# Local attention in 64-row windows: sending the last unit out in two stores, and asking for its v one store earlier

## The chip, the cores and the metric

One core of one Trainium2 chip. The time is device microseconds of one execution. Runs were "fast" (one core, so the only test is that no run lies over 1.5% above the fastest of its kernel).

## The reference

q, k and v are float32 of shape (4, 4096, 1536). The sequence is cut into windows of 64 rows; each window attends to itself alone.

```python
logits = np.einsum('bnwd,bnud->bnwu', q_w, k_w) * D ** -0.5
attn = np.exp(logits - logits.max(-1, keepdims=True))
attn = attn / attn.sum(-1, keepdims=True)
out = np.einsum('bnwu,bnud->bnwd', attn, v_w)
```

## The kernel before

The 16,384 rows go through in 32 units of 512 rows. Each unit's q, k and v are loaded by GpSimd's queue, cast to float16 on the way, into landing buffers two deep. GpSimd copies them on, and asks for the load two units ahead at each copy ("hand_over"). TensorE transposes q and k, multiplies, ScalarE takes exponentials, TensorE multiplies by v, and VectorE and ScalarE share the evictions, which also divide by the sums. A partition holds four consecutive rows of the unit, 24,576 bytes, which leave in one piece. All stores but the last are issued by GpSimd, on the same queue as the loads; the last is issued by SyncE.

```python
def hand_over(x, u, dst, m, g):
    gp.wait_ge(landed[x][u % NL], ...)      # the load of unit u has landed
    gp.wait_ge(m, u)                        # unit u-1 no longer reads dst
    gp.tensor_copy(out=dst, in_=landing[x][u % NL])
    ...
    request(x, u + NL)                      # NL = 2: the load two units ahead
...
for u in range(1, N):                       # GpSimd
    hand_over("q", u, q16, m_q, g_q)
    hand_over("k", u, k16, m_k, g_k)
    gp.wait_ge(m_q, u + 1)                  # unit u-1 is evicted
    store(u - 1)
    hand_over("v", u, v16, m_v, g_v)

for a in range(2):                          # SyncE: n_e counts the evictions of
    sy.wait_ge(n_e[a], 3)                   # rows 2 and 3 of the last unit
sy.dma_start(out=rows(of, (N - 1) * UR, SLOTS, SLOTS),
             in_=slots(outs[(N - 1) % NO], 0, SLOTS, SLOTS)).then_inc(d_l, 16)
```

The softmax here doesn't subtract the row's maximum and nothing guards it: scores larger than these inputs give would overflow.

## Time and profile before

| | before |
|---|---|
| median of 6 runs | 943.4 us (943.28 to 944.1) |
| span of the profiled run | 941.3 us |
| busiest compute engine (PE) | 68% |
| DMA engines busy | nine tenths or more in 39 of 40 slices |
| HBM read and written | 428 GB/s over the span |
| last eviction ends, last store issued | 929.21, 929.24 us |

The prediction shows the lines themselves (in them PE is TensorE, PEld its weight loads, DVE VectorE, ACT ScalarE, POOL GpSimd and SP SyncE; the granted clock is a share of TensorE's full clock). They are to be read from the DMA row downwards: the compute engines have room to spare, and after the start the only stretch before the end in which most DMA engines have nothing to do is 928 to 930 us (DMA share 0.28).

### The profile page before, as it was taken

How to read it: one execution, taken by the hardware profiler on the slowest of the kernel's cores; microseconds unless marked ns; L12 is line 12 of the kernel's file. 1: busy time of each engine (PE TensorE's matmuls, PEld its weight loads, DVE VectorE, ACT ScalarE, POOL GpSimd, SP SyncE). 2: the span in 40 equal slices, each digit the busy share in tenths (PEclk: the TensorE clock that was granted, in tenths of full speed). 3: DMA queues.
4: the chain of work that ended last, by engine and by line, in shares of the span. 5: the costliest groups of instructions: out<-in, count | busy, mean ns of one | idle time of the engine just before them, and what ended most of it. 6: DMA issues, size and time to landing. Idle time of an engine off the chain costs nothing. (4 is left out here: it accounts for less than half of the span.)

```text
span 941.3 us, 13141 instructions
## 1 busy us (share of the span) xinstructions
PE 641.9 (68%) x5120; PEld 371.9 (40%) x3584; DVE 288.4 (31%) x517; ACT 336.0 (36%) x642; POOL 334.1 (35%) x225
## 2 busy tenths in 40 slices
PE   0877777666767767768676586676866767757673
PEld 0544444432444433444233442344533444323440
DVE  0233333332323333233322233222333223322232
ACT  0344444333333233333333333333334334233331
POOL 4244433344333342333423334333343333443220
PEclk9999999998889888797888999889789789888997
DMA  9999999999999999999999999999999999999997
GB/s 257 217 216 279 264 237 282 284 279 276 233 275 283 281 281 237 266 282 282 281 245 257 283 281 282 255 246 283 283 280 264 237 284 283 280 277 230 276 320 329
DMA packets 22540, 253.35 MB, mean 269 GB/s; under 512 B 2048, under 2 KB 2048, under 8 KB 10240
## 3 DMA queue, kind: packets, MB, share of 16 engines
q0 software_dynamic: 22240, 246.95, 99.7%
q1 hardware_dynamic: 288, 6.29, 1.7%
q14 instruction: 10, 0.08, 0.0%
q8 instruction: 2, 0.03, 0.0%
HBM read 301.99 MB, written 100.66 MB: 428 GB/s over the span
## 5 line engine op out<-in xcount | busy, mean ns | idle before, releaser
L164 PE MATMUL lt<-xq,xk 128*128 128x256 f16 x1536 | 203.3, 282 | 0.0
L300 POOL COPY v<-vl 128x3072 f32<-128x3072 f32 x31 | 85.2, 2748 | 278.3 <-DMA vl<-in_v_dram 278.3
L192 PEld LDWEIGHTS <-et 128*64 128x64 f16 x512 | 40.5, 131 | 331.6 <-issue 319.4
L152 PE MATMUL tp<-ident,k 128*128 128x128 f32 x768 | 124.9, 297 | 57.9 <-PEq L218 40.5
L164 PEld LDWEIGHTS lt<-xq,xk 128*128 128x128 f16 x1536 | 153.2, 100 | 27.3
L152 PE MATMUL tp<-ident,q 128*128 128x128 f32 x768 | 107.9, 285 | 80.1 <-DVE xq L228 55.8
L112 PE MATMUL sp<-ones,et 128*64 128x1 f16 x512 | 52.6, 178 | 147.8 <-PEq L218 130.6
L152 PEld LDWEIGHTS tp<-ident,q 128*128 128x128 f32 x768 | 85.9, 145 | 120.8 <-issue 120.7
L228 ACT COPY xk<-tp 128x512 f32<-128x512 f32 x96 | 59.6, 620 | 203.2 <-ACTq L218 203.2
L152 PEld LDWEIGHTS tp<-ident,k 128*128 128x128 f32 x768 | 96.0, 152 | 75.1 <-issue 73.1
L300 POOL COPY k<-kl 128x3072 f32<-128x3072 f32 x31 | 85.2, 2748 | 103.1 <-DMA kl<-in_k_dram 103.1
L245 DVE RECIPROCAL rs<-sp 128x1 f32<-128x1 f32 x128 | 21.4, 167 | 323.8 <-DVEq L218 323.2
L300 POOL COPY q<-ql 128x3072 f32<-128x3072 f32 x31 | 85.0, 2743 | 100.0 <-DMA ql<-in_q_dram 99.9
L228 DVE COPY xk<-tp 128x512 f32<-128x512 f32 x96 | 66.5, 693 | 168.2 <-DVEq L218 168.2
L112 PE MATMUL o<-v,et 128*64 128x512 f16 x768 | 117.7, 440 | 0.0
L279 ACT ACTIVATE out<-tp,rs 128x512 f32<-128x512 f32 x64 | 44.0, 687 | 177.4 <-ACTq L218 177.4
L269 ACT ACTIVATE et<-lt,zeros 32x128 f16<-32x128 f32 x256 | 92.0, 359 | 39.4 <-ACTq L218 36.1
L228 ACT COPY xq<-tp 128x512 f32<-128x512 f32 x96 | 56.3, 586 | 126.4 <-ACTq L218 126.4
L112 PE MATMUL tp<-v,et 128*64 128x512 f16 x512 | 100.2, 468 | 0.0
L256 DVE TENSOR_SCALAR out<-o,rs 128x512 f32<-128x512 f32 x128 | 90.4, 747 | 28.6 <-DVEq L218 28.6
L228 DVE COPY xq<-tp 128x512 f32<-128x512 f32 x96 | 66.1, 688 | 83.7 <-DVEq L218 83.7
L112 PE MATMUL lt<-v,et 128*64 128x512 f16 x256 | 64.5, 479 | 0.0
(21 smaller groups left out, 217.6 us busy)
## 6 DMA issues: line engine op xcount, KB each, us to landing
out_dram<-out POOLq DMA_DIRECT2D x31, 3072.0 KB, 61.6
ql<-in_q_dram POOLq DMA_DIRECT2D x31, 1536.0 KB, 54.9
kl<-in_k_dram POOLq DMA_DIRECT2D x31, 1536.0 KB, 54.9
vl<-in_v_dram POOLq DMA_DIRECT2D x31, 1536.0 KB, 54.9
out<-in_q_dram SPq DMA_DIRECT2D x1, 3072.0 KB, 16.7
out_dram<-out SPq DMA_DIRECT2D x1, 3072.0 KB, 10.7
k<-in_k_dram POOLq DMA_DIRECT2D x1, 1536.0 KB, 17.9
v<-in_v_dram POOLq DMA_DIRECT2D x1, 1536.0 KB, 24.3
```

The lines of the kernel that those rows point to most:

```text
L112: return nc.tensor.add_instruction(mybir.InstMatmult(name=nc.get_next_instruction_name(), engine=PE, ins=[low(rhs), low(w)], outs=[low(o)] ...
L152: ins = nc.tensor.transpose(tps[g % 2][:, r, j, :], pairs[:, c * P : (c + 1) * P], ident[:, :])
L164: ins = nc.tensor.matmul(lts[h][:, r, :, :], lhsT=keys(c, h, r, w), rhs=queries(c, h, w), start=(c == 0 and w == 0 and r == 0), stop=(c == ...
L192: ld = nc.tensor.ldweights(w[h], tile_position=(0, P // H * h))
L228: copy(out=dst, in_=tps[g % 2][:, :, :, :]).then_inc(f_c[g % 4], 1)
L245: ve.reciprocal(out=rs[:, n : n + 1], in_=sp[:, n : n + 1]).then_inc(n_d, 1)
L256: ins = ve.tensor_scalar_mul(scaled(u, n, j), bank(n, j), scalar1=rs[:, n : n + 1])
L269: ins = sc.activation(ets[h][s, :, :, t], lts[h][s, :, :, t], EXP, bias=zeros[s, 0:1], scale=scale)
L279: ins = sc.activation(scaled(u, n, j), bank(n, j), COPY, bias=0.0, scale=rs[:, n : n + 1])
L300: gp.tensor_copy(out=dst[:, :, :].bitcast(FP32), in_=landing[x][u % NL][:, :, :].bitcast(FP32)).then_inc(c_l, 1)
```

## The change

The intent is to close that stretch in two ways. The last unit's v is requested ahead of a store that stood in front of it in the queue, so that the last unit can be computed sooner; and the first two rows of the last unit go out while the last two are still computed. The diff, cut to its core:

```diff
         for u in range(1, N):
             hand_over("q", u, q16, m_q, g_q)
             hand_over("k", u, k16, m_k, g_k)
+            if u + NL == N - 1:
+                hand_over("v", u, v16, m_v, g_v)
             gp.wait_ge(m_q, u + 1)
             store(u - 1)
-            hand_over("v", u, v16, m_v, g_v)
-        for a in range(2):
-            sy.wait_ge(n_e[a], 3)
-        sy.dma_start(
-            out=rows(of, (N - 1) * UR, SLOTS, SLOTS), in_=slots(outs[(N - 1) % NO], 0, SLOTS, SLOTS)
-        ).then_inc(d_l, 16)
+            if u + NL != N - 1:
+                hand_over("v", u, v16, m_v, g_v)
+        last = rows(of, (N - 1) * UR, SLOTS, SLOTS)[:, 0, :]
+        for i, c in enumerate((1, 3)):
+            for a in range(2):
+                sy.wait_ge(n_e[a], c)
+            sy.dma_start(
+                out=last[:, 2 * i * D : 2 * (i + 1) * D],
+                in_=outs[(N - 1) % NO][:, 2 * i : 2 * (i + 1), :].rearrange("p r d -> p (r d)"),
+            ).then_inc(d_l[i], 16)
```

(`d_l` becomes two semaphores, and the end waits for both.)

More of the change, by code (lines that the diff above doesn't have):

```diff
@@ L76 @@
     d_o = [sem(f"d_o{i}") for i in range(NO)]
-    d_l = sem("d_l")
+    d_l = [sem(f"d_l{i}") for i in range(2)]
     g_q, g_k, g_v = (sem(n) for n in ("g_q", "g_k", "g_v"))
@@ L381 @@
             sy.wait_ge(d_o[i], 16 * (last // NO + 1))
-        sy.wait_ge(d_l, 16)
+        for i in range(2):
+            sy.wait_ge(d_l[i], 16)
         lo, hi = min(s.num for s in sems), max(s.num for s in sems)
```

## The prediction

> **What bounds the kernel now.** I read the page first, for the occupancy of each engine and of the DMA engines, then the page's DMA queues and issues.
>
> ```profile
> PE 641.9 (68%) x5120; PEld 371.9 (40%) x3584; DVE 288.4 (31%) x517; ACT 336.0 (36%) x642; POOL 334.1 (35%) x225
> ...
> DMA  9999999999999999999999999999999999999997
> ...
> q0 software_dynamic: 22240, 246.95, 99.7%
> q1 hardware_dynamic: 288, 6.29, 1.7%
> ...
> HBM read 301.99 MB, written 100.66 MB: 428 GB/s over the span
> ```
>
> No compute engine is above 68%, while the 16 DMA engines are full in 39 of 40 slices. This is a copy-bound kernel: each unit of 512 rows moves three loads and one store of 3.15 MB each, and the steady rhythm in the timeline is 29.3 us a unit (v copies at 829.34, 858.61, 887.90). So what matters is only when the DMA engines have nothing to do. That can be at the start, which the change leaves alone, and at the end. I therefore cut the end into stretches (columns: stretch, its length, busy us of PE, PE weight load, DVE, ACT, POOL, granted clock, DMA share, GB/s).
>
> ```profile
> 25.00:925.00 900.00, 637.61 (x5088) 369.94 (x3570) 284.16 (x507) 332.29 (x637) 323.45 (x211) 0.89 1.02 269
> 925.00:928.00 3.00, 2.67 (x28) 0.40 (x6) 1.89 (x6) 1.63 (x4) 0.00 (x0) 1.00 0.94 401
> 928.00:930.08 2.08, 0.00 (x0) 0.00 (x0) 1.21 (x2) 0.49 (x1) 0.00 (x0) 1.00 0.28 118
> 930.08:937.50 7.42, 0.00 (x0) 0.00 (x0) 0.00 (x0) 0.00 (x0) 0.00 (x0) 0.59 0.99 418
> 937.50:938.60 1.10, 0.00 (x0) 0.00 (x0) 0.00 (x0) 0.00 (x0) 0.00 (x0) 0.50 0.16 67
> ```
>
> The reader sees a hole: from 928 to 930.08 the DMA share drops to 0.28, because the queue of earlier work runs dry and the last store is not yet issued. The timeline of the same place says why:
>
> ```profile
> 902.45 2.75 POOL L300 COPY k<-kl 128x3072 f32<-128x3072 f32 x1 [4.52 <-DMA kl<-in_k_dram]
> ...
> 905.82 0.54 POOL L285 DMA_DIRECT2D out_dram<-out  x1 [0.62 <-POOL k L300]
> ...
> 915.38 2.98 ACT L269 ACTIVATE et<-lt,zeros 32x128 f16<-32x128 f32 x8 [1.13 <-ACTq L218]
> 917.14 2.75 POOL L300 COPY v<-vl 128x3072 f32<-128x3072 f32 x1 [10.78 <-DMA vl<-in_v_dram]
> 920.05 0.14 PEld L192 LDWEIGHTS <-et 128*64 128x64 f16 x2 [4.18 <-issue]
> ...
> 926.21 0.75 DVE L256 TENSOR_SCALAR out<-tp,rs 128x512 f32<-128x512 f32 x1 [0.45 <-DVEq L218]
> 926.22 0.69 ACT L279 ACTIVATE out<-tp,rs 128x512 f32<-128x512 f32 x1 [1.04 <-ACTq L218]
> ...
> 927.80 1.41 DVE L256 TENSOR_SCALAR out<-o,rs 128x512 f32<-128x512 f32 x2 [0.45 <-DVEq L218]
> 927.81 0.69 ACT L279 ACTIVATE out<-o,rs 128x512 f32<-128x512 f32 x1 [0.32 <-ACTq L218]
> 929.24 0.35 SPq L373 DMA_DIRECT2D out_dram<-out  x1
> ```
>
> The last v lands at 917.1, is copied, the second product starts at 920.05, its last eviction ends at 927.80 + 1.41 = 929.21, and only then does the one 3 MB store go out.
>
> The share is an average over 16 engines, so I went to the records of the single DMA packets. A packet of 24,576 B takes 0.91 us; each engine has 8 of a store. Between 25 and 925 us I find no idle moment on any of the 16 engines (longest gap 0.08 us). At the end they part. The 16 closing records of the last software-queue store come at 927.84, 927.95, 927.96 and so on; the 13th at 929.89, the 14th and 15th at 930.36 and 930.37, the 16th at 931.61. The last store's packets start at 930.08. So 13 engines stand idle before it, for 0.18 to 2.37 us, 22.3 engine-microseconds together; three engines never stand idle. The one that finishes its old work at 931.61 ends the program: 13 of the last store's closing records fall in 937.41 to 937.57, two at 938.18 and 938.45, and this engine's at 939.46; the issue view has 10.7 us from issue to landing, so landing at 939.94. This engine did not catch up during the hole, because it had no hole: its lag on the quickest is 1.75 us at 19 us, 2.52 at 500 and 3.77 at 931.6.
>
> **What the Trainium skill says.** "DMA: Bandwidth & Descriptors", section "Issuing engines are not separate DMA queues", says that transfers issued from different engines run on the same 16 DMA engines and interleave. The trace agrees: the hardware-queue packets follow the software-queue ones on the same chains. The same page, "Queues, rings and completion order", says that each DMA engine takes turns between its queues at packet granularity; around 930.4 two packets that overlap a software-queue one last 1.46 and 1.73 us instead of 0.91, which fits. Its section "Why a DMA increments its semaphore by 16 and not by 1" says that only the full 16 means that all data have landed. That is the core of this prediction: the latest engine counts, not the mean. Its section "Latency and other measured facts" says that two of the engines are usually slower in traces; the trace shows one that trails, though the records carry no engine number to compare.
>
> **The change part by part.**
>
> (1) *The last v asked for ahead of a store.* In the unit whose v copy starts at 858.61, GpSimd now issues the load of the last v (861.95 before) ahead of the store that it issued at 847.75. The software queue is served in order and is some 55 us deep (median landing of loads 54.9 us), so the late issue does not starve it; the two transfers change places. Each takes 7.3 us of queue (8 x 0.91), so the last v lands near 909.8 instead of 917.1. What then holds the product is the exponentials: they end at 915.38 + 2.98 = 918.36, against the v copy's 917.14 + 2.75 = 919.89. The gain is 920.05 - 918.4 = 1.6 to 1.7 us on the last eviction, not 7.3. The displaced store lands 7.3 us later, at about 917.2, and the first eviction of the last unit needs its buffer; that would be at 921.86 - 1.6 = 920.2, so about 3 us are in hand.
>
> (2) *The last store in two.* The first half waits for the first evictions of row 2 (926.21 + 0.75 = 926.96, and 926.22 + 0.69 = 926.91) instead of 929.21, so 2.25 us earlier, with part (1) at about 925.3. From the start of issue to the first packet it took 930.08 - 929.24 = 0.84 us, so first packets come near 926.2, before the quickest engine runs dry at 927.84. The second half is ready near 927.6, with packets near 928.5; by then the first half's 8 packets of about 0.46 us (3.65 us) are still being worked off until 927.84 + 3.65 = 931.5. So the hole closes completely: 22.3 engine-microseconds of idleness vanish.
>
> (3) *What it costs.* Each engine gets 16 packets of 12,288 B instead of 8 of 24,576. From v loads, whose packets read 12,288 B and take 0.47 us, 16 x 0.47 = 7.5 against 8 x 0.91 = 7.3, so 0.2 us on every engine. One more store issue (0.35 us) on SyncE falls while transfers run; one more satisfied wait at the end is an estimate of under 0.1 us.
>
> *The sum.* On the quick engines, the end moves from 937.5 to 927.84 + 7.5 = 935.3, a gain of 2.2. On the slowest, which sets the time, no idleness is removed: 931.61 + 7.5 = 939.1. Before, it ended at 939.47, which is 931.61 + 7.3 plus about 0.58: an instruction fetch of 8,192 B at 933.43 (0.31 us) and the packet after it that took 1.18 us. If the fetch comes again at this engine, 939.1 becomes 939.7; if not, or if the work is ordered more kindly, 939.1. Against 939.47 that is -0.4 to +0.2. I put the middle, -0.15, on the median: 943.36 - 0.15 = 943.2.
>
> **The rivals.** *The hole is on the path.* Then the time falls by up to 2.2 us, to about 941.2, and with a second-slowest engine at the end something between. For it: DMA share of 0.28 just before the last store. Against it: the three engines that end last were not idle there. It would hold if in unprofiled runs the engines trailed less than in the profile; but to have even 1 us of gain the slowest must finish its old work by 929.1, which is 2.5 us earlier than here, and then the unprofiled runs of before would be faster than the profiled one. They are 943.29 to 944.1, the profiled 943.07. *The displaced store becomes a wait.* If it lands over 3 us later than worked out, evictions of the last unit start late and the second half goes out late. Even 2 us would still be covered by queued transfers (the slowest has work until 931.61), so the time stays within 0.5 us, 943.9 at most. *Smaller packets or sharing cost more than the loads show*: at twice my overhead, +0.2 us more, 943.6. *The load order pays 7.3 us*: this would need the last unit's chain to begin with v; the exponentials at 918.36 speak against it, and the total of bytes still has to pass: at best the same 941.2.
>
> **Range and chances.** The mechanism gives 942.9 to 943.6; runs of before spread by 0.8 us, and a partial gain of the first rival is possible, so 942.3 to 944.1. Two per cent would be 18.9 us, more than eight times the length of the hole; so 98% within it.
>
> **What would show it.** Right: the DMA share near 1.0 between 928 and 930 instead of 0.28, two SyncE stores about 2.2 us apart with the first near 925.3, the second product starting near 918.4 and the last v copy near 909.9; then a ragged end, most engines done near 935.3 to 937.8 with the share falling from about 935, one alone to 939.1 to 939.7; span 940.9 to 941.5. Wrong: a span under 940, with no engine trailing alone by over 2 us at the end; or a hole that is still there; or the last unit's evictions waiting on their buffer, which would be a start after 921.

## The result, and the profile after

The changed kernel takes 943.7 us in the median of 6 runs (943.44 to 943.84), the kernel before 943.4 (943.28 to 944.1) on the same chip: ratio 1.0001, 95% interval 0.9988 to 1.0014. Ratios here are the mean time of one kernel's fast runs over that of the other's in the same rounds, so not quite the ratio of the medians. There is no difference that these runs can see.

And yet the profile shows that the change did all that it was meant to do. First the timeline of the changed kernel (start, length, engine, line, operation, idle time before it and what ended that):

```profile
909.92 2.75 POOL L300 COPY v<-vl 128x3072 f32<-128x3072 f32 x1 [3.43 <-DMA vl<-in_v_dram]
...
917.48 0.20 PE L112 MATMUL sp<-ones,et 128*64 128x1 f16 x2 [2.31 <-ACT et L269]
...
924.86 2.56 SPq L379 DMA_DIRECT2D out_dram<-out  x2
...
925.65 1.41 DVE L256 TENSOR_SCALAR out<-o,rs 128x512 f32<-128x512 f32 x2 [0.45 <-DVEq L218]
```

The last v is copied from 909.92 instead of 917.14, and the last product, no longer waiting for v but for the exponentials ("ACT et"), starts at 917.48 instead of 920.20 (its first weights, at 920.05 in the prediction's line, are loaded from 917.41). The last eviction ends at 927.06 instead of 929.21, and the first half of the last unit goes out at 924.86, 4.4 us before the whole store of the kernel before. Now the stretches of the end, in the columns of the prediction's view:

```profile
925.00:928.00 3.00, 0.52 (x6) 0.00 (x0) 1.58 (x3) 1.02 (x2) 0.00 (x0) 0.97 0.95 410
928.00:930.08 2.08, 0.00 (x0) 0.00 (x0) 0.00 (x0) 0.00 (x0) 0.00 (x0) 0.50 0.97 414
930.08:935.00 4.92, 0.00 (x0) 0.00 (x0) 0.00 (x0) 0.00 (x0) 0.00 (x0) 0.50 1.01 429
935.00:937.50 2.50, 0.00 (x0) 0.00 (x0) 0.00 (x0) 0.00 (x0) 0.00 (x0) 0.50 0.37 157
937.50:938.60 1.10, 0.00 (x0) 0.00 (x0) 0.00 (x0) 0.00 (x0) 0.00 (x0) 0.50 0.08 34
938.60:941.70 3.10, 0.00 (x0) 0.00 (x0) 0.00 (x0) 0.00 (x0) 0.00 (x0) 0.50 0.02 8
```

The hole is gone: the DMA share between 928 and 930.08 is 0.97, where it was 0.28. The idle time has moved to the other side of the store, where it is of no use to anyone: from 935 on the share is 0.37, then 0.08, then 0.02, which is a third of one engine of 16. In the records of the single packets, 15 engines end between 935.40 and 937.58, and one at 939.92; before, 15 ended between 937.42 and 938.45, and one at 939.46. The quick engines gained up to 2 us. The slow one gained nothing, and the kernel ends with it. (The records carry no engine number. But a packet's record starts 3 to 4 ns before the record ahead of it on its engine ends, and a record of 4 bytes, the "closing record", ends each engine's share of a transfer; by these two marks the packets can be chained. Times are counted from the same zero as in the views.)

### The profile page after: what moved, and what is told of

The parts are those of the page before. It is cut to its first block, busy times and chain, and to the rows that moved or that the text cites. A ratio compares the mean times of both kernels' runs of the same rounds, so it can differ in the third digit from the quotient of the medians.

```text
span 941.7 us, 13144 instructions
## 1 busy us (share of the span) xinstructions
PE 644.9 (68%) x5120; PEld 373.5 (40%) x3584; DVE 288.3 (31%) x517; ACT 335.5 (36%) x642; POOL 334.2 (35%) x225
```

## The experiments

The theory on trial, S: every DMA engine has its own list of work, no engine is idle in the middle of the kernel, and the end is that of the engine with the longest list. Its rivals: C, closing the hole does gain 2 us but the change gives them back elsewhere; H, the hole is on the path, and any shift of the last store shifts the end; M, the sum of bytes over all engines sets the end. Each run below had five rounds beside the kernel before, whose medians on these chips were 943.06 to 943.56 us.

### Each part alone: split_only and order_only

split_only: the order of the requests as before, the last store in two.

```diff
-            if u + NL == N - 1:
-                hand_over("v", u, v16, m_v, g_v)
             gp.wait_ge(m_q, u + 1)
             store(u - 1)
-            if u + NL != N - 1:
-                hand_over("v", u, v16, m_v, g_v)
+            hand_over("v", u, v16, m_v, g_v)
```

> The last store in two halves, the last v not moved ahead. Theory S (the DMA engine that trails the others and never stands idle sets the end): the first half goes out near 927.0, the hole shrinks to little or nothing, and the time stays at 943.4 to 943.8, since the trailing engine's last packet stays near 939.5 to 939.9. Rival C (closing the hole does gain 2 us, and the displaced store of the other part gives it back): 941.3 to 942.0.

order_only: the other way round, in the kernel before.

```diff
+            if u + NL == N - 1:
+                hand_over("v", u, v16, m_v, g_v)
             gp.wait_ge(m_q, u + 1)
             store(u - 1)
-            hand_over("v", u, v16, m_v, g_v)
+            if u + NL != N - 1:
+                hand_over("v", u, v16, m_v, g_v)
```

> The last v ahead of a store, the last store whole. Theory S: the store goes out about 2 us earlier (near 927.2, as the last evictions in the changed kernel end at 927.06), the hole shrinks to a few tenths, and the time stays at 943.1 to 943.7. Rival C, now with the cost in the smaller packets of the two halves: without them the gain of 1.5 to 2 us would show, 941.5 to 942.0.

Measured: split_only 943.1 us, ratio 1.0000 (0.9986 to 1.0014); order_only 943.51 us, ratio 1.0005 (0.9992 to 1.0019). The store's issue and one stretch of order_only:

```profile
925.05 0.35 SPq L376 DMA_DIRECT2D out_dram<-out  x1
```

```profile
928.00:930.08 2.08, 0.00 (x0) 0.00 (x0) 0.00 (x0) 0.00 (x0) 0.00 (x0) 0.50 1.02 441
```

This is the plainest case. One whole store, with the packets of the kernel before, goes out 4.2 us earlier (925.05 against 929.24; I had expected 2, the exponentials and evictions of this run were early too), the hole is fully closed, and the slowest engine ends at 939.68 against 939.46. (It was 0.49 us further back at the closing of the store before, 924.55 against 924.05.) In split_only the hole is closed to a share of 0.82:

```profile
928.00:930.08 2.08, 0.48 (x6) 0.00 (x0) 1.58 (x3) 0.99 (x2) 0.00 (x0) 1.00 0.82 349
```

Its slowest engine ends at 939.10, and its median is 0.3 us under the range given for S, within the noise. Rival C falls: neither part has a gain that the other could give back.

### The last store later: late6 and late6_changed

If the slowest engine still has old work when the store's packets come, a later store must cost nothing at first and then cost one for one. late6 puts six evictions that no one needs between VectorE's last eviction and the last store of the kernel before.

```diff
+        if u == N - 1:
+            for i in range(6):
+                ve.tensor_scalar_mul(
+                    xq[:, i, :], bank(H * R - 1, NJ - 1), scalar1=rs[:, 3:4]
+                ).then_inc(n_e[0], 1)
...
-            sy.wait_ge(n_e[a], 3)
+            sy.wait_ge(n_e[a], 3 if a else 9)
```

> The kernel before with six idle evictions of about 0.7 us on VectorE put between its last eviction and the last store, so the store goes out 4.2 us later and the hole is made 4.2 us wider. Theory S: the trailing engine had 931.61 - 930.08 = 1.5 us of old work left when the store's packets came, so only 4.2 - 1.5 = 2.7 us reach the time: 945.8 to 946.4. Rival H (the hole is on the path for all engines): the full 4.2 us, 947.5.

Measured: 946.77 us, ratio 1.0035 (1.0022 to 1.0049), which is 3.3 us (2.1 to 4.6); the medians on this chip are 3.7 us apart. That is 0.4 us above the range given for S. The delay as the timeline has it, and two stretches:

```profile
930.28 4.03 DVE L262 TENSOR_SCALAR xq<-o,rs 128x512 f32<-128x512 f32 x6
...
934.34 0.35 SPq L378 DMA_DIRECT2D out_dram<-out  x1
```

```profile
930.08:935.00 4.92, 0.00 (x0) 0.00 (x0) 4.23 (x7) 0.00 (x0) 0.00 (x0) 0.75 0.02 10
935.00:937.50 2.50, 0.00 (x0) 0.00 (x0) 0.00 (x0) 0.00 (x0) 0.00 (x0) 0.50 1.12 472
```

In this run the evictions before the added ones were also about 1.1 us later, so the store went out 5.1 us later than in the kernel before, not 4.2. H then says 5.1; S says 5.1 less the 1.5 us of old work, 3.6. The time agrees with S and excludes 5.1, if the other executions had the delay of the profiled one; the 4.2 us that H had been given beforehand it would not exclude. The packets decide: the slowest engine closed its old work at 931.94, all 16 then stood idle until 935.18 (DMA share 0.02), and its first packet of the store came 3.56 us later than in the kernel before (931.62), not 5.1. The other 15 end within 942.53 to 942.66, and one at 943.24.

late6_changed puts the same six evictions before the second half of the changed kernel.

```diff
-                sy.wait_ge(n_e[a], c)
+                sy.wait_ge(n_e[a], c if a or c == 1 else 9)
```

(and the six evictions as above)

> The changed kernel with the same six idle evictions (4.03 us on VectorE in the earlier run) ahead of its second half. The half goes out near 926.3 + 4.0 = 930.3 to 931.5, its packets come near 931 to 932.5. Theory S: the trailing engine still works on old packets and the first half until about 931.6 + 3.7 = 935.3, so nothing of the delay reaches the time: 943.3 to 944.0. Rival H, that whatever delays the last store delays the end: 947 to 948, as in the delayed kernel before, which rose by 3.3 us.

Measured: 943.52 us, ratio to the kernel before 0.9999 (0.9986 to 1.0013). Beside it on the same chip the changed kernel ran once more.

> The changed kernel once more, as the partner of the next run on the same chip: 943.3 to 943.9, the slowest engine's last packet 2 us or more after the second slowest.

It took 943.6 us (ratio 1.0001), its slowest engine ended at 940.31 and the second slowest at 937.93. The delay in late6_changed, and the stretch at the hole:

```profile
926.28 6.51 SPq L384 DMA_DIRECT2D out_dram<-out  x2
```

```profile
928.00:930.08 2.08, 0.00 (x0) 0.00 (x0) 2.08 (x4) 0.00 (x0) 0.00 (x0) 0.79 0.86 366
930.08:935.00 4.92, 0.00 (x0) 0.00 (x0) 2.34 (x4) 0.00 (x0) 0.00 (x0) 0.50 0.92 389
```

The row of the issues spans both halves, from 926.28 to 932.79. The same delay that cost the kernel before 3.3 us costs the changed one nothing. In the packet records eleven engines wait for the second half and go on at 933.28 to 933.43, while those of the slowest engine follow each other without a gap from 927.01 to its end. (The profiled execution was the slowest of its five, 944.91 us; the other four were 943.23 to 943.53. Its slowest engine was 1.0 us behind that of after_again at the closing of the store before, 926.03 against 925.03, so before the delay could act.) So the change is not without effect: what it bought is slack of four microseconds or more for the last evictions, of which this kernel had no need.

### More work for some of the engines: one8 and low4

If the longest list sets the end, a little work on one engine must cost nearly its full length. one8 adds eight loads of one row at the start, into the third output buffer, which is free until unit 2.

```diff
+        src = rows(qf, 0, SLOTS, SLOTS)[:, 0, :]
+        for i in range(8):
+            nc.sync.dma_start(
+                out=outs[2][i : i + 1, :, :].rearrange("p r d -> p (r d)"),
+                in_=src[i : i + 1, :],
+            ).then_inc(d_x, 16)
```

(and a wait for them before that buffer is given free)

> The changed kernel with eight extra loads of one row of 24,576 B each at the start, into a buffer that is not in use yet: meant for one DMA engine alone, 8 x 0.91 = 7.3 us of extra work on it, 0.08% of all bytes. Theory S (the engine with the most work sets the end, and the lag persists because no engine is ever idle): that engine ended at 935.4 to 937.5 if it is not the trailing one (939.88), so it now ends at 942.7 to 944.8 and the time rises by 2.8 to 5 us, to 946.5 to 948.7; by 7.3 us to 951 if it is the trailing one. Rival M (the sum over all engines sets the end): 7.3 / 16 = 0.5 us, 944.2.

Measured: 946.07 us, ratio 1.0028 (1.0014 to 1.0042), 2.6 us above the kernel before and 2.4 above the changed one's earlier median: 0.4 us under the lowest value of S, five times the value of M. The issue, and the end of one8:

```profile
out<-in_q_dram SPq DMA_DIRECT2D x8, 24.0 KB
```

```profile
937.50:940.00 2.50, 0.00 (x0) 0.00 (x0) 0.00 (x0) 0.00 (x0) 0.00 (x0) 0.50 0.12 49
940.00:944.00 4.00, 0.00 (x0) 0.00 (x0) 0.00 (x0) 0.00 (x0) 0.00 (x0) 0.50 0.05 22
```

Two engines of 16 are left after 937.88, one to 941.14 and one to 942.47. Nine hundred microseconds after those eight rows were loaded, their 7.3 us were still missing on one engine: 942.47 less the 7.4 us that the last store takes is 935.1, and the quickest engine closed its old store at 927.77, 7.3 us before. Nothing in the kernel lets an engine catch up, because its list never runs empty. That 0.08% more bytes cost 0.28% is not to be explained by the sum. Nor by the last store: its halves were issued 3.6 us later than in the changed kernel (928.49 against 924.86), but the engine that ends last had old packets until 936.98 and shows no gap from 919 to its end.

low4 meant to put half that work on each of eight engines.

```diff
+        for i in range(4):
+            nc.sync.dma_start(
+                out=outs[2][8 * i : 8 * i + 8, :, :].rearrange("p r d -> p (r d)"),
+                in_=src[8 * i : 8 * i + 8, :],
+            ).then_inc(d_x, 16)
```

> The changed kernel with four extra loads of eight rows of 24,576 B at the start, meant for eight of the engines, 4 x 0.91 = 3.65 us of extra work on each. Theory S: if the trailing engine is among the eight, the time rises by 3.65 us to 947.3; if it is among the other eight, the best-placed of the loaded ones ends at 935.4 + 3.65 = 939.0 and the worst at 937.5 + 3.65 = 941.2 against 939.88, so the rise is 0 to 1.3 us, 943.7 to 945.0. Rival M: 3.65 / 2 = 1.8 us, 945.5 in either case.

Measured: 952.88 us (4 runs), ratio 1.0106 (1.0091 to 1.0122), far above what either theory said. The premise failed: the 32 added packets took 2.13 us in the mean, not 0.91. Each load went to eight neighbouring partitions, from eight engines at a time. The Trainium skill, "SBUF — State Buffer", section "Door 1: The DMA port swizzle", says that DMA bandwidth depends on how many of the 16 ports the partitions reach, and that four neighbours share one; slow packets agree with that, though no run here varied the partitions alone. At the end eight engines were 6.9 us or more behind the quickest, the last unit came later with them (its first half went out at 933.51), and the other eight stood idle for 3.0 to 4.9 us before it:

```profile
928.00:935.00 7.00, 5.88 (x54) 0.86 (x12) 4.04 (x10) 3.97 (x6) 0.00 (x0) 0.89 0.70 300
```

It fits S in kind, not in size, and it doesn't decide anything that one8 had not decided.

### A last store on 15 engines: fifteen

The changed kernel, with the last unit divided so as to leave one engine out.

```diff
-                out=last[:, 2 * i * D : 2 * (i + 1) * D],
+                out=last[:120, 2 * i * D : 2 * (i + 1) * D],
...
+        sy.dma_start(out=last[120:127, :], in_=src[120:127, :]).then_inc(d_l[2], 16)
+        sy.dma_start(out=last[127:128, :]...).then_inc(d_l[3], 16)
```

> The changed kernel, with the last unit stored so that 15 DMA engines carry it: partitions 0 to 119 in the two halves, 120 to 126 in one store, 127 in one. If the division goes as the records of other stores suggest, the 16th engine gets nothing and low-numbered ones get about 1 packet of 24,576 B more (0.9 us). Theory S: if the 16th is the one that trails, its work ends near 934 or before, the second slowest (937.5) sets the end, and the time falls by about 2.3 us to 941.4; if the trailing one is among the low-numbered, it gets 0.9 us more and the time rises to 944.6; if it is another, no change. Rival M (the sum of bytes over all engines sets the end, whichever engine carries them): no change, 943.7, in any case.

Measured: 946.56 us, ratio 1.0029 (1.0015 to 1.0042); none of the three values. One engine did get nothing, and it was the quickest: the packet records show it done at 928.63, with the first closing of the last old store. And the other 15 were slowed, for the packets of 12,288 B took 0.571 us in the mean (up to 1.85, though half of them still 0.460), where they take 0.460 in the changed kernel:

```profile
928.00:930.08 2.08, 0.00 (x0) 0.00 (x0) 0.00 (x0) 0.00 (x0) 0.00 (x0) 0.50 0.87 317
930.08:935.00 4.92, 0.00 (x0) 0.00 (x0) 0.00 (x0) 0.00 (x0) 0.00 (x0) 0.50 0.91 302
```

The share is 0.91, but only 302 GB/s move, where 429 moved in the same stretch of the changed kernel. So a share near 1 does not mean full speed. This run decides nothing between the theories; the way to lighten the slow engine was not found. No version here beats the two kernels.

## Why the prediction was right, by its steps

It gave 943.2 us, 942.3 to 944.1, and 98% within two per cent; measured were 943.7 and ratio 1.0001. The nearness of the number shows little, since anyone who expected no change would have said 943.4; what was tested is why nothing comes of closing the hole. Two of the signs that it named missed by 0.2 us: the span is 941.7 (941.5 at most was said), and the slowest engine ends at 939.92 (939.7).

- **No engine is idle before the end; the hole is 13 engines' and not the slowest one's.** Held. order_only and late6 are the two sides of it: the store 4.2 us earlier leaves the end of the last packet within 0.22 us (later, not earlier), the store 5.1 us later moves it by 3.78.
- **Part (1): v near 909.8, the product at 918.4, held by the exponentials.** The v copy started at 909.92. The product waited for the exponentials as said, but started at 917.48, because those themselves ended 1.0 us earlier (914.39 + 2.97 = 917.36). The granted clock differs from run to run in this place (0.83 between 906 and 910 us, where the run of before had 0.69), which may be why; it was not tested. The last eviction gained 2.15 us, where 1.6 to 1.7 had been worked out.
- **The displaced store is no wait.** Held: the first evictions follow the product, at 919.74, where 920.2 had been worked out and a start after 921 would have shown the wait.
- **Part (2): first half issued near 925.3, its packets near 926.2.** This step failed. The half was issued at 924.86; but its first packets came at 928.09, after 3.2 us, not 0.84. That term was taken from a store that met idle engines. On full ones, some old packets went first. The hole closed all the same, and that was luck, with nothing to spare: the quickest engine closed its old store at 928.08.
- **Part (3): 0.2 us for smaller packets.** Over-sized. 16 packets of 12,288 B take 16 x 0.460 = 7.36 us against 7.30; 0.06 us. I had taken the casting loads for the measure.
- **The slowest engine at 939.1 to 939.7.** It came at 939.92. It was 0.57 us further back already at the closing of the store before (924.63, against 924.05). And of the two branches the later one came true: the instruction fetch fell on this engine again (930.19, 0.31 us, and the packet after it took 1.20 us instead of 0.91). It falls on the slowest engine in the records of six of the eight experiments too; in one8 no fetch comes after 882, and in fifteen it cannot be followed. In late6, where all 16 engines start the last store together, the engine with the fetch ends last, 0.6 us after the next.
- **The sum: -0.4 to +0.2 us.** The measured difference is within the noise of these runs, about 0.13% or 1.2 us either way, so its sign is not settled; a gain of 2 us is excluded.

Two readings in the prediction's packet records do not hold, though nothing rests on them. The two packets of 1.46 and 1.73 us near 930.4 start 6 ns after the closing record of their own engine, so no old packet was left there to take turns with; the turns do show in the changed kernel (closing list below). And the lag of 2.52 us at 500 us is not one engine's: two engines have it there, and a third 2.04.

What stays open is why one engine trails. In the kernel before, the last closing of a transfer comes about 2.5 us after the first from 280 to 724 us; after that one engine falls back alone, to 3.77 us. It does so only in stores, by about 0.15 us in each from 760 to 877 us, with packets at 0.94 to 0.99 us where others take 0.91, and in no load. The instruction fetches before the end (406.6, 697.4, 877.8) don't do it: its lag does not change at them. The records carry no engine number. What an even division would give can only be estimated: in the changed kernel the mean end of the 16 engines is 936.3, so some 3.6 us, 0.4%.

## What to carry to other kernels

A busy share over 16 DMA engines says how much work there is, not who ends last; before closing a hole at the end, look in the packet records whether the engine that ends last has the hole at all. A delay that lies in the shadow of other work costs nothing until it outgrows the shadow, and closing it gains nothing either; shifting the last transfer both ways, as order_only and late6 do, finds that edge with two runs. Where queues are kept full from start to end, a microsecond lost by one engine at the start is still missing at the end.

## What the Trainium skill lacked or had wrong

- "DMA: Bandwidth & Descriptors", section "Queues, rings and completion order": taking turns between queues packet by packet is what the slowest engine of the changed kernel shows once begun (its last old packets start 1.37 us apart, 0.91 + 0.46). The page does not say what comes before: a store issued on full engines had its first packet after 3.2 us (2.8 in order_only), against 0.84 in the kernel before, in split_only and in late6, where quick engines had run dry.
- The same page, section "Anatomy of one DMA — SWDGE (gpsimd) path", puts most of about 2 us of fixed cost between the last byte and the semaphore. In the kernel before, the last software-queue store landed about 0.5 us after the last engine's closing record (905.82 + 26.3 against 931.61), and the hardware-queue one about 0.5 us after its own (929.24 + 10.7 against 939.46). That speaks against the page only if the records end with the last byte, which no run here shows.
- The same page, section "Latency and other measured facts", calls engines 7 and 15 the usually slower ones. If a transfer over 15 engines leaves out the 16th, as the page's rule for the number of engines says (section "Why a DMA increments its semaphore by 16 and not by 1"), then in the run fifteen that engine was the quickest of all (done at 928.63), and another one trailed.
- "SBUF — State Buffer", section "Door 1: The DMA port swizzle", has no figure for a transfer that ill suits the ports beside full queues: 2.13 us instead of 0.91 for a packet of 24,576 B in low4, and 0.571 in the mean instead of 0.460 for 12,288 B in fifteen, if that is the cause there too.
- No page that I read says that DMA engines which are always full drift apart and stay apart (the last 1.75 us behind the first at 19 us, 3.77 at the end of the kernel before).
